# HGRN2 scores as sixteen 32x32 diagonal chunks, and values multiplied chunk by chunk

## The chip, the cores and the metric

The kernel runs on one core of one Trainium2 chip. The metric is the device time of one execution in microseconds (us). A core has a matrix engine (TensorE, PE in the profile, with its weight loads as PEld), VectorE (DVE), ScalarE (ACT), GpSimd (POOL) and SyncE (SP), which here issues most DMA transfers. Each engine works through its own list of instructions in order; semaphores tie the lists together. PE reads SBUF and writes PSUM, which has eight banks.

## The reference

The program is a two-layer encoder trunk on 512 tokens of 1024 features. Each layer projects the normalised input, sends the columns through four mixers side by side (Hyena, Mamba2, dilated attention, HGRN2), projects their outputs back and adds them; then comes a mixture of 16 experts. The change touches HGRN2 alone, whose core is a gated linear attention in chunks of 32 tokens, run once forwards and once backwards, with 4 heads of 64:

```
q, k, v, g = rs(q), rs(k), rs(v), rs(g)          # 16 chunks of 32 tokens
gc = jnp.cumsum(g, axis=2)
ref = gc[:, :, H_CHUNK // 2 - 1:H_CHUNK // 2]
scores = jnp.einsum("bclhe,bcshe->bchls", q * jnp.exp(gc - ref), k * jnp.exp(ref - gc))
scores = jnp.where(mask, scores, 0.0)            # mask: lower triangle, 32 x 32
o_intra = jnp.einsum("bchls,bcshp->bclhp", scores, v)
...
o_inter = jnp.einsum("bclhe,bchep->bclhp", q * jnp.exp(gc), prev)
return (o_intra + o_inter).reshape(b, L, h, pd)
```

Scores join only tokens of one chunk; what comes from earlier chunks comes through the state `prev`. The two directions are added, normalised and gated.

## The kernel before

The 512 tokens stand in four blocks of 128 (b = 0 to 3), each with four chunks of 32 (cc = 0 to 3). The 256 HGRN2 features stand in two halves i of 128 partitions, each with two heads h of 64. The function `hgrn` goes over i. For a half it first prepares the decayed q and k of both directions e (`hgrn_decay`: tiles gqk, and gqi for the part that meets the state), turns k (line 1133), makes the chunk states (1141) and scans them over the chunks on VectorE (1151, 1153) into gR.

Then, for each head h, it makes the scores of each direction: four matmuls of 128x128, one for a block, into one PSUM bank (line 1162, tile gsc). Only the four 32x32 squares on the diagonal of each 128x128 result are wanted. GpSimd clears a page (1164, tile gP), VectorE copies the wanted entries into it under the mask `hmask` (1165), and adds the pages of the two directions (1168). For each block, one matmul with 128 rows multiplies the page with the values of the block (1171), which opens the sum in the output bank go, and for each of its chunks one or two matmuls add the state's part (1178): these have 64 rows (the head's features) and 32 columns (the chunk's tokens), so that the four chunks of a block use four separate column strips of PE's array. The first chunk has no state before it and the last none behind it.

All matmuls here are fp32. In the trace each leaves two records of a weight load and two of a matmul.

The order of the work: `hgrn` is a generator that yields weights, and `weave` interleaves it with `mamba_proj`, the projection for the next mixer (lines 395 to 397 and 417 to 419, tiles pcm and ptm), 40 against 31. A scheduler turns the program into a list for each engine, so the yields move where projection matmuls stand between those of `hgrn`. There is no other table of orders for this stage. After the mixers of a layer, `pieces` streams the expert weights (tile we, line 1391) on the SP queue into buffers that the mixers gave up.

Of the kernel before, what the change touches and what calls it, by code (L numbers as in the profile page):

```python
# [20 lines left out]
P = 128  # L21
# [17 lines left out]
def shape_constants():  # L39
    f32 = np.float32  # L40
    p = np.arange(P)
    c = np.zeros((P, C_N), f32)
    c[:, C_ID:C_ID + P] = np.eye(P)
    c[:, C_LE:C_LE + P] = p[:, None] <= p[None, :]
    c[:, C_GE:C_GE + P] = p[:, None] >= p[None, :]
    c[:, C_IOTA:C_IOTA + 64] = np.arange(1, 65)
    c[:, C_TOK:C_TOK + 4] = 2 * (P * np.arange(4)[None, :] + p[:, None])
    c[:, C_HALF] = p >= 64
    c[:, C_KEY] = 1.0 / KEY
    c[:, C_KEY + 1] = 1.0  # L50
    c[:, C_SLOT] = p % 64 + 1
    same = (p[:, None] // 32) == (p[None, :] // 32)
    m = np.zeros((P, 2, P), np.int32)
    m[:, 0] = same & (p[:, None] <= p[None, :])
    m[:, 1] = same & (p[:, None] >= p[None, :])

    eo = np.concatenate([np.arange(0, L, 2), np.arange(1, L, 2)])
    f = 2.0 * np.pi * (np.arange(P, dtype=np.float64) + 0.5) / (2 * L)  # L60
    n = np.arange(L).reshape(P, 4).T
    th = n[:, :, None] * f
    dft = np.stack([np.cos(th), np.sin(th)]).astype(f32)
    idft = np.ascontiguousarray(dft.transpose(0, 1, 3, 2))
    tk = [eo[:, None] * f, eo[:, None] * (np.pi / 2 - f)]
    kdft = np.stack([np.concatenate([np.cos(tk[0]), np.cos(tk[1])], axis=1),
                     np.concatenate([np.sin(tk[0]), -np.sin(tk[1])], axis=1)])
    kdft = (kdft * (2.0 / (2 * L))).astype(f32)

    t = np.linspace(0.0, 1.0, L, dtype=f32)[:, None]  # L70
    ang_pos = (f32(2.0 * math.pi) * np.arange(L, dtype=f32) / f32(L)).astype(f32)
    bands = np.linspace(1e-4, 15, 16, dtype=f32)
    ang = (ang_pos[:, None] * bands[None, :]).astype(f32)
    z = np.concatenate([t, np.cos(ang), -np.sin(ang)], axis=-1).astype(f32)
    lo = math.log(1e-2) / 1.5
    hi = math.log(1e-2) / 0.3
    deltas = np.abs(np.linspace(lo, hi, 256, dtype=f32))
    decay = np.exp(-t * deltas[None, :]).astype(f32)[eo]

    d = np.arange(511, -512, -1)  # L80
    n = np.abs(d)
    nf = np.maximum(n, 1).astype(f32)
    large = 8 + (np.log(nf / f32(8)) / f32(math.log(128.0)) * f32(8)).astype(np.int32)
    bucket = (d > 0) * 16 + np.where(n < 8, n, np.minimum(large, 15))
    mult = (n <= 64).astype(int) + ((n <= 256) & (n % 4 == 0)) + (n % 16 == 0)
    oh = np.zeros((33, 1024), f32)
    oh[bucket, np.arange(1023)] = 1.0
    oh[32, :1023] = np.where(mult > 0, np.log(np.maximum(mult, 1)), -1e30)
    return {
        "c_pack": c, "c_hmask": m, "c_dft": dft, "c_idft": idft, "c_kdft": kdft,  # L90
        "c_zT": np.ascontiguousarray(z.T), "c_decay": decay, "c_bucket": oh,
    }
# [18 lines left out]
def encoder(ctx: ExitStack, tc: tile.TileContext, d, out, dbg=None, stages=None, nlayers=NL):  # L111
    nc = tc.nc
    V, A, G, T, SY = nc.vector, nc.scalar, nc.gpsimd, nc.tensor, nc.sync
# [33 lines left out]
    def bank_b(name):  # L147
        return tagged(psb, "b", [512], F32, name)

    def page(shape, name, dt=F32):  # L150
        return tl("G", shape, name, dt)
# [68 lines left out]
    ps = bank_b("nmT")  # L220
# [896 lines left out]
    def hgrn(l, st, cols, lb):  # L1117
        q, f, v, g = st
        ve = hgrn_values(v)
        keep = page([2, L], "keep", BF)  # L1120
        G.memset(keep, 1.0)
        G.memset(keep[:, 0, 0::32], 0.0)
        G.memset(keep[:, 1, 31::32], 0.0)
        yield 2
        po = [bank_b("go") for _ in range(2)]
        pov = [p.rearrange("p (b i c) -> p b i c", b=4, i=2) for p in po]
        for i in range(2):
            qk, qi, bes = yield from hgrn_decay(l, i, q, f, lb, keep)
            R = [tl("B", [64, 16], "gR") for _ in range(2)]
            for e in range(2):  # L1130
                ps = bank_b("gkT")
                for b in range(4):
                    T.transpose(ps[:, b * P:(b + 1) * P], qk[1][:, e, b * P:(b + 1) * P], ident)
                kT = page([4, P], "gkT")
                A.activation(kT, ps.rearrange("p (b c) -> p b c", b=4), AF.Copy)
                pu = [bank_b("gU") for _ in range(2)]
                for b in range(4):
                    for z in range(2):
                        a = slice(64 * z, 64 * z + 64)
                        for h in range(2):  # L1140
                            T.matmul(pu[z][64 * h:64 * h + 64, b * P:(b + 1) * P], kT[a, b, 64 * h:64 * h + 64],
                                     ve[b][a, 2 * i + h], start=True, stop=True)

                U, w = tl("B", [64, 16], "gU"), tl("B", [64, 16], "gw")
                for z in range(2):
                    A.activation(U.rearrange("p n (b z c) -> p z b c n", z=2, c=2)[:, z],
                                 pu[z].rearrange("p (b c n) -> p b c n", b=4, n=64), AF.Copy)
                A.activation(w, bes[e][:, None, :].to_broadcast([P, 64, 16]), AF.Copy)
                u, r, w = (x.rearrange("p n c -> p (n c)") for x in (U, R[e], w))
                if e == 0:  # L1150
                    V.tensor_tensor_scan(r, w, u, 0.0, ALU.mult, ALU.add)
                else:
                    V.tensor_tensor_scan(r[:, ::-1], w[:, ::-1], u[:, ::-1], 0.0, ALU.mult, ALU.add)
                yield 2.5
            for h in range(2):
                s = slice(64 * h, 64 * h + 64)
                Ps = []
                for e in range(2):
                    ps = bank_b("gsc")
                    for b in range(4):  # L1160
                        c = slice(b * P, (b + 1) * P)
                        T.matmul(ps[:, c], qk[1][s, e, c], qk[0][s, e, c], start=True, stop=True)
                    w = page([4, P], "gP")
                    G.memset(w, 0.0)
                    V.copy_predicated(w, hmask[:, e, None, :].to_broadcast([P, 4, P]),
                                      ps.rearrange("p (b c) -> p b c", b=4))
                    Ps.append(w)
                V.tensor_add(Ps[0], Ps[0], Ps[1])
                yield 2
                for b in range(4):  # L1170
                    T.matmul(pov[h][:, b, i], Ps[0][:, b], v[:, b, (2 * i + h) * 64:(2 * i + h + 1) * 64],
                             start=True, stop=False)
                    for cc in range(4):
                        c = 4 * b + cc
                        for e in range(2):
                            p = c - 1 if e == 0 else c + 1
                            if 0 <= p < 16:
                                T.matmul(pov[h][32 * cc:32 * cc + 32, b, i], qi[s, e, 32 * c:32 * c + 32],
                                         R[e][s, :, p], start=False, stop=(e == 1 or c == 15))
                    yield 0.8  # L1180
        gs = tl("B", [4, 256], "ggs")
        silu_inplace(g, gs, gs)
        y = tl("B", [4, 256], "gy")
        ss = small([2, 8], "gss")
        for h in range(2):
            sq = page([8, 64], "gsq")
            A.activation(sq, po[h].rearrange("p (n c) -> p n c", c=64), AF.Square)
            V.reduce_sum(ss[:, h], sq, axis=AX.X)
        r = small([16], "grr")
        rsqrt(r, ss.rearrange("p h n -> p (h n)"), 64, "g")  # L1190
        for h in range(2):
            yv = y.rearrange("p b (i h c) -> p b i h c", i=2, h=2)[:, :, :, h]
            V.tensor_mul(yv, pov[h],
                         r.rearrange("p (h b i) -> p h b i", h=2, b=4)[:, h, :, :, None].to_broadcast([P, 4, 2, 64]))
        V.tensor_mul(y, y, gs)
        mix_tile(3)
        for i in range(2):
            ps = bank_b("gyT")
            for b in range(4):
                T.transpose(ps[:, b * P:(b + 1) * P], y[:, b, i * P:(i + 1) * P], ident)  # L1200
            mix_put(3, i, ps, cols[:, R_HGN:R_HGN + 1])
        yield 4
# [432 lines left out]
```

## Time and profile before

| what | value |
|---|---|
| three timed runs | 1661.7, 1661.99, 1667.71 us (median 1661.99) |
| the profiled execution | 1665.74 us, span 1664.0 us |
| granted PE clock, mean over the span | 0.972 of full |
| PE busy | 1536.9 us (92%), 8899 matmul records |
| VectorE busy | 805.7 us (48%) |
| ScalarE, GpSimd busy | 396.1 us, 214.0 us |
| DMA | 468.55 MB, mean 282 GB/s |

The span runs from the first to the last instruction. Busy time of PE counts its pipelined records, whose ends are modelled, so two records can overlap and a busy PE need not be at its peak. The stages lie twice in the span, once for each layer: norm and HGRN2 projection, HGRN2 with Mamba2's projection, Mamba2 with Hyena's, Hyena with attention's, attention, router, experts. PEclk is the clock that PE was granted: 1.00 stands for 2.4 GHz and 0.50 for 1.2 GHz.

### The profile page before, as it was taken

To read this page: it belongs to the slowest core of one execution; us is meant where nothing else is said; L and a number is where in the kernel's file an instruction comes from. 1 tells how busy PE (TensorE), PEld (TensorE's weight loads), DVE (VectorE), ACT (ScalarE), POOL (GpSimd) and SP (SyncE) were. 2 spreads that over 40 slices of the span, in tenths; PEclk is the share of its full clock that TensorE was granted. 3 is DMA by queue.
4 is the path that set the end of the run, shared out by engine and by line. 5 is a ranking of instruction groups with operands and counts; after the bars stand their busy time and mean duration, and the time that the engine had idled before them with its cause. 6 is when DMAs were issued, how large, how long until landed. Compare 5 with 4: busy or idle time off the path is not lost.

```text
span 1664.0 us, 22783 instructions
## 1 busy us (share of the span) xinstructions
PE 1536.9 (92%) x8899; PEld 879.6 (53%) x8899; DVE 805.7 (48%) x1727; ACT 396.1 (24%) x805; POOL 214.0 (13%) x214
## 2 busy tenths in 40 slices
PE   7989999989999998998889999999899999999985
PEld 6778788763433433332368788787534433332332
DVE  6777777562433342331266767856533433332323
ACT  4344434430001010000152435243200001000012
POOL 3232132000000000000033232300000000000001
PEclk9989999989999999999989889999899999999998
DMA  5411224679999999999912202167799999999995
GB/s 165 129 51 28 75 76 162 237 265 369 421 419 422 420 421 420 420 422 420 385 54 80 74 26 77 55 231 261 256 402 419 420 421 420 421 420 420 420 421 239
DMA packets 153486, 468.55 MB, mean 282 GB/s; under 512 B 20408, under 2 KB 56664, under 8 KB 144418
## 3 DMA queue, kind: packets, MB, share of 16 engines
q1 hardware_dynamic: 144742, 455.10, 69.8%
q0 software_dynamic: 2240, 7.34, 1.1%
q10 hardware_dynamic: 6396, 4.65, 0.8%
q8 instruction: 70, 1.15, 0.3%
q14 instruction: 38, 0.31, 0.0%
HBM read 460.60 MB, written 6.44 MB: 281 GB/s over the span
## 4 chain that ended last, share of the span: by engine, by line
PE 61%; DMA 25%; DVE 6%; ACT 3%; issue 2%; POOL 2%; ACTq 0%; SPq 0%; DVEq 0%; POOLq 0%
DMA we<-in_moe_w_up_dram 10%; PE eg L1399 9%; DMA we<-in_moe_w_down_dram 7%; PE eu L1399 7%; PE ey L1399 7%; DMA we<-in_moe_w_gate_dram 6%; PE pcm L395 3%; PE pcm L396 3%; PE pcm L397 3%; PE ec L1470 3%; PE po L1220 2%; PE po L1221 2%; PE po L1222 2%; PE ptm L418 2%; PE ptm L417 2%
## 5 line engine op out<-in xcount | busy, mean ns | idle before, releaser
L1399 PE MATMUL eu<-we,exT 128*64 128x512 f32 x1024 | 239.4, 599 | 20.3 <-DMA we<-in_moe_w_up_dram 18.4
L1399 PE MATMUL ey<-we,ehT 128*64 128x512 f32 x1024 | 232.9, 598 | 18.8 <-ACT ehT L1435 11.5
L1399 PE MATMUL eg<-we,exT 128*64 128x512 f32 x1024 | 231.2, 597 | 10.6 <-DMA we<-in_moe_w_gate_dram 5.9
L1399 PEld LDWEIGHTS eu<-we,exT 128*64 128x64 f32 x1024 | 67.0, 136 | 187.2 <-issue 87.9
L1301 DVE SCALAR_TENSOR_TENSOR ra<-er,ra,tie 128x512 bf16<-128x512 f32 x128 | 95.9, 749 | 135.4 <-PE er L1309 132.5
L1399 PEld LDWEIGHTS ey<-we,ehT 128*64 128x64 f32 x1024 | 69.0, 136 | 157.9 <-issue 96.3
L1399 PEld LDWEIGHTS eg<-we,exT 128*64 128x64 f32 x1024 | 68.8, 136 | 151.4 <-issue 107.3
L1452 DVE SCALAR_TENSOR_TENSOR eY<-ey,erg,eY 64x512 fp32r<-64x512 f32 x64 | 48.0, 749 | 205.3 <-ACT eY L1451 205.2
L1420 ACT ACTIVATE eh<-eg 128x512 f32<-128x512 f32 x32 | 19.1, 598 | 505.3 <-PE eg L1399 505.3
L397 PE MATMUL pcm<-hT,whl 128*128 128x512 f32 x320 | 128.9, 403 | 3.5 <-DVE whl L381 3.5
L396 PE MATMUL pcm<-hT,whl 128*128 128x512 f32 x320 | 130.3, 407 | 0.0
L395 PE MATMUL pcm<-hT,whl 128*128 128x512 f32 x320 | 130.1, 406 | 0.0
L1471 DVE TENSOR_TENSOR x<-x,ec 128x512 f32<-128x512 f32 x128 | 79.8, 682 | 102.8 <-PE ec L1470 102.8
L1346 POOL DMA_INDIRECT exe<-xd,erow x28 | 27.8, 994 | 783.2 <-DVE erg L1327 526.6
L1451 ACT ACTIVATE eY<-ey,erg 64x512 fp32r<-64x512 f32 x64 | 43.7, 683 | 269.4 <-PE ey L1399 245.0
L1427 DVE TENSOR_TENSOR eh<-eh,eu 128x512 f32<-128x512 f32 x32 | 22.0, 688 | 158.7 <-PE eu L1399 158.7
L417 PE MATMUL ptm<-wtm,hT 128*128 128x256 f32 (+1 forms) x256 | 76.5, 300 | 1.7 <-DVE aqs L924 1.7
L1470 PE MATMUL ec<-eY,eot 128*128 128x512 f32 x256 | 67.3, 405 | 10.2 <-DVE erow L1344 6.4
L418 PE MATMUL ptm<-wtm,hT 128*128 128x256 f32 (+1 forms) x256 | 74.6, 293 | 1.3 <-DVE wtm L381 1.3
L380 POOL TENSOR_SCALAR whl<-wraw 128x1024 fp32r<-128x1024 f32 x40 | 46.7, 1169 | 222.1 <-PE pcm L397 113.8
L419 PE MATMUL ptm<-wtm,hT 128*128 128x256 f32 (+1 forms) x256 | 73.7, 291 | 0.0
L397 PEld LDWEIGHTS pcm<-hT,whl 128*128 128x128 f32 x320 | 62.4, 195 | 18.3 <-DVE whl L381 3.9
(386 smaller groups left out, 2381.4 us busy)
## 6 DMA issues: line engine op xcount, KB each, us to landing
we<-in_moe_w_gate_dram SPq DMA_DIRECT2D x216, 512.0 KB
we<-in_moe_w_up_dram SPq DMA_DIRECT2D x208, 512.0 KB
we<-in_moe_w_down_dram SPq DMA_DIRECT2D x204, 512.0 KB
wraw<-in_w_in_dram SPq DMA_DIRECT2D x27, 1024.0 KB
we<-in_moe_w_down_dram SPq DMA_DIRECT2D x26, 1024.0 KB
we<-in_moe_w_up_dram SPq DMA_DIRECT2D x24, 1024.0 KB
we<-in_moe_w_gate_dram SPq DMA_DIRECT2D x20, 1024.0 KB
wo<-in_w_out_dram SPq DMA_DIRECT2D x8, 1024.0 KB
```

Source lines behind the costliest of these rows:

```text
L380: G.tensor_scalar(dst_hi, raw, 1.0, 0.0, op0=ALU.mult, op1=ALU.add)
L395: T.matmul(ps, w[:, 0, k, :], H[k], start=(k == 0), stop=False)
L396: T.matmul(ps, w[:, 0, k, :], Lo[k], start=False, stop=False)
L397: T.matmul(ps, w[:, 1, k, :], H[k], start=False, stop=(k == 7))
L417: T.matmul(dst, h, w[:, 0, k % 4], start=(k == 0), stop=False)
L418: T.matmul(dst, h, w[:, 1, k % 4], start=False, stop=False)
L419: T.matmul(dst, g, w[:, 0, k % 4], start=False, stop=(k == 7))
L1301: V.scalar_tensor_tensor(g, pr, ra[:, c, e, 0:1], tie[:, 384 - c * P:896 - c * P], op0=ALU.subtract, op1=ALU.is_gt, accum_out=k)
L1399: T.matmul(ps[f][64 * f:64 * f + 64], xT[:, j, h], qs[4 * h + j][:, f * 512:(f + 1) * 512], start=(h == 0 and j == 0), stop=(h == 1 and j ...
L1452: V.scalar_tensor_tensor(lo, src, w[c, 0:1], hi.bitcast(F32), op0=ALU.mult, op1=ALU.subtract)
L1470: T.matmul(ps, ot[:, t * P:(t + 1) * P], Y[i][q][n], start=(q == 0), stop=(q == 1))
L1471: V.tensor_add(xrow(t)[:, c], xrow(t)[:, c], ps)
```

## The change

The scores are computed for the sixteen 32x32 squares alone, for each head and direction: 64 matmuls of 64 rows, 32 columns and 32 moving columns for a half i, in place of 16 matmuls of 128x128. Both heads are done in one go. A head has one bank now, with direction e in columns 128 e to 128 e + 127: chunk cc of block b lies on partitions 32 cc to 32 cc + 31, in columns 32 b to 32 b + 31. So the bank is packed, one page w holds both heads and both directions, there are two masked copies of 256 columns and one addition for a half, and the mask is laid out to match.

The page has no zeros between chunks any more, so the value matmul goes chunk by chunk: 32 rows (the chunk's tokens), 32 columns, 64 moving columns, on the row and column strip cc. Each is followed by the state matmuls of its chunk. The yields change from 2 + 4 x 0.8 for a head to 3 for a half and 4 x 1 for a head.

```diff
@@ -49,10 +49,10 @@
     c[:, C_KEY] = 1.0 / KEY
     c[:, C_KEY + 1] = 1.0
     c[:, C_SLOT] = p % 64 + 1
-    same = (p[:, None] // 32) == (p[None, :] // 32)
-    m = np.zeros((P, 2, P), np.int32)
-    m[:, 0] = same & (p[:, None] <= p[None, :])
-    m[:, 1] = same & (p[:, None] >= p[None, :])
+    m = np.zeros((P, 2, 4, 32), np.int32)
+    m[:, 0] = ((p % 32)[:, None] <= np.arange(32))[:, None]
+    m[:, 1] = ((p % 32)[:, None] >= np.arange(32))[:, None]
+    m = m.reshape(P, 2, P)
@@ -1152,32 +1152,37 @@
                 else:
                     V.tensor_tensor_scan(r[:, ::-1], w[:, ::-1], u[:, ::-1], 0.0, ALU.mult, ALU.add)
                 yield 2.5
+
+            pc = [bank_b("gsc") for _ in range(2)]
+            for e in range(2):
+                for c in range(16):
+                    b, cc = divmod(c, 4)
+                    t = slice(32 * c, 32 * c + 32)
+                    for h in range(2):
+                        s = slice(64 * h, 64 * h + 64)
+                        T.matmul(pc[h][32 * cc:32 * cc + 32, P * e + 32 * b:P * e + 32 * b + 32], qk[1][s, e, t],
+                                 qk[0][s, e, t], start=True, stop=True)
+            w = page([2, 2, P], "gP")
+            G.memset(w, 0.0)
+            for h in range(2):
+                V.copy_predicated(w[:, h], hmask, pc[h][:, :256].rearrange("p (e c) -> p e c", e=2))
+            V.tensor_add(w[:, :, 0], w[:, :, 0], w[:, :, 1])
+            yield 3
             for h in range(2):
                 s = slice(64 * h, 64 * h + 64)
-                Ps = []
-                for e in range(2):
-                    ps = bank_b("gsc")
-                    for b in range(4):
-                        c = slice(b * P, (b + 1) * P)
-                        T.matmul(ps[:, c], qk[1][s, e, c], qk[0][s, e, c], start=True, stop=True)
-                    w = page([4, P], "gP")
-                    G.memset(w, 0.0)
-                    V.copy_predicated(w, hmask[:, e, None, :].to_broadcast([P, 4, P]),
-                                      ps.rearrange("p (b c) -> p b c", b=4))
-                    Ps.append(w)
-                V.tensor_add(Ps[0], Ps[0], Ps[1])
-                yield 2
                 for b in range(4):
-                    T.matmul(pov[h][:, b, i], Ps[0][:, b], v[:, b, (2 * i + h) * 64:(2 * i + h + 1) * 64],
-                             start=True, stop=False)
                     for cc in range(4):
                         c = 4 * b + cc
+                        t = slice(32 * cc, 32 * cc + 32)
+                        o = pov[h][t, b, i]
+                        T.matmul(o, w[t, h, 0, 32 * b:32 * b + 32], v[t, b, (2 * i + h) * 64:(2 * i + h + 1) * 64],
+                                 start=True, stop=False)
                         for e in range(2):
                             p = c - 1 if e == 0 else c + 1
                             if 0 <= p < 16:
-                                T.matmul(pov[h][32 * cc:32 * cc + 32, b, i], qi[s, e, 32 * c:32 * c + 32],
-                                         R[e][s, :, p], start=False, stop=(e == 1 or c == 15))
-                    yield 0.8
+                                T.matmul(o, qi[s, e, 32 * c:32 * c + 32], R[e][s, :, p], start=False,
+                                         stop=(e == 1 or c == 15))
+                    yield 1
         gs = tl("B", [4, 256], "ggs")
         silu_inplace(g, gs, gs)
         y = tl("B", [4, 256], "gy")
```

On PE, at the scores of the first half in the first layer, the list before was as follows (gU the chunk states, gsc_1102 and gsc_1110 the two directions of head 0, pcm the projection):

```order
L1141 MATMUL gU_1079<-gve_895,gkT_1076 64x128 x2
L1162 MATMUL gsc_1102<-gqk_956,gqk_957 128x128 x4
L1162 MATMUL gsc_1110<-gqk_956,gqk_957 128x128 x4
L396 MATMUL pcm_1125<-hT_127,whl_1122 128x512
L397 MATMUL pcm_1125<-hT_123,whl_1122 128x512
```

In the list of the changed kernel the same place begins like this (gsc_1102 is head 0, gsc_1103 head 1):

```order
L1141 MATMUL gU_1079<-gve_895,gkT_1076 64x128 x2
L1163 MATMUL gsc_1102<-gqk_956,gqk_957 32x32
L1163 MATMUL gsc_1103<-gqk_956,gqk_957 32x32
L1163 MATMUL gsc_1102<-gqk_956,gqk_957 32x32
L1163 MATMUL gsc_1103<-gqk_956,gqk_957 32x32
```

The two heads alternate, 64 matmuls in a row, before the projection goes on.

At the first value block, still on PE, before (go_954 is the output bank of head 0, gR_1038 and gR_1039 the states of the two directions, gsc_1195 a score bank of head 1):

```order
L397 MATMUL pcm_1125<-hT_124,whl_1122 128x512
L1171 MATMUL go_954<-gv_260,gP_1107 128x64
L1162 MATMUL gsc_1195<-gqk_956,gqk_957 128x128 x3
L1178 MATMUL go_954<-gR_1039,gqi_958 32x64
L1178 MATMUL go_954<-gR_1038,gqi_958 32x64
L1178 MATMUL go_954<-gR_1039,gqi_958 32x64
L1178 MATMUL go_954<-gR_1038,gqi_958 32x64
L1178 MATMUL go_954<-gR_1039,gqi_958 32x64
L1178 MATMUL go_954<-gR_1038,gqi_958 32x64
L1178 MATMUL go_954<-gR_1039,gqi_958 32x64
L1171 MATMUL go_954<-gv_260,gP_1107 128x64
```

The same block in the changed kernel's list on PE, where L1178 is now the value matmul of a chunk and L1183 the state matmul:

```order
L397 MATMUL pcm_1264<-hT_121,whl_1261 128x512
L1178 MATMUL go_954<-gv_260,gP_1168 32x64
L1183 MATMUL go_954<-gR_1039,gqi_958 32x64
L1178 MATMUL go_954<-gv_260,gP_1168 32x64
L1183 MATMUL go_954<-gR_1038,gqi_958 32x64
L1183 MATMUL go_954<-gR_1039,gqi_958 32x64
L1178 MATMUL go_954<-gv_260,gP_1168 32x64
```

One value matmul stood ahead of the state matmuls of four chunks; now one stands ahead of those of each chunk, and this goes on for the 16 chunks of a head. In the first half of a layer projection matmuls stand between the two heads; in the second half the 16 chunks of head 1 follow those of head 0 directly.

## Rows read from the trace of the kernel before

**Rows 1.** The page: busy time by engine, and the chain that ended last.

```profile
PE 1536.9 (92%) x8899; PEld 879.6 (53%) x8899; DVE 805.7 (48%) x1727; ACT 396.1 (24%) x805; POOL 214.0 (13%) x214
...
PE 61%; DMA 25%; DVE 6%; ACT 3%; issue 2%; POOL 2%; ACTq 0%; SPq 0%; DVEq 0%; POOLq 0%
```

**Rows 2.** Windows by stage: busy us and count by engine, PE clock, DMA, GB/s.

```profile
95.00:198.00 103.00, 94.86 (x814) 77.26 (x813) 81.09 (x143) 42.60 (x72) 26.30 (x28) 0.90 0.17 52
...
912.00:1014.00 102.00, 96.70 (x805) 78.91 (x803) 74.04 (x129) 40.23 (x66) 25.95 (x24) 0.88 0.17 53
...
345.00:835.00 490.00, 453.86 (x2389) 182.98 (x2387) 166.82 (x415) 59.80 (x121) 25.78 (x30) 0.99 0.99 400
1165.00:1664.00 499.00, 449.97 (x2375) 181.78 (x2373) 171.24 (x427) 62.28 (x120) 29.02 (x32) 0.98 0.96 390
```

**Rows 3.** Waits of the SP queue, 198 to 345: total us, times, longest.

```profile
SPq L1391 <- PE alog L967: 16.4, 5, 14.2
```

**Rows 4.** Waits of PE for masked scores, 905 to 1160: total us, times, longest.

```profile
PE go L1171 <- DVE gP L1168: 3.8, 2, 2.7
```

**Rows 5.** Timeline of PE, first layer: start, length, line, rows x columns, count.

```profile
127.84 0.43 PE L1171 MATMUL go<-gv,gP 128*128 128x64 f32 x2
128.20 0.67 PE L1178 MATMUL go<-gR,gqi 64*32 64x64 f32 x16
128.80 0.43 PE L1171 MATMUL go<-gv,gP 128*128 128x64 f32 x2
...
130.11 0.65 PE L1178 MATMUL go<-gR,gqi 64*32 64x64 f32 x14
130.69 0.49 PE L1162 MATMUL gsc<-gqk,gqk 64*128 64x128 f32 x2
```

**Rows 6.** The same, start of a whole value block and what follows it.

```profile
137.62 0.33 PE L1171 MATMUL go<-gv,gP 128*128 128x64 f32 x2
...
141.30 0.39 PE L417 MATMUL ptm<-wtm,hT 128*128 128x264 f32 x1
```

**Rows 7.** The same, a piece of a value block of the second layer at half clock.

```profile
940.77 0.69 PE L1171 MATMUL go<-gv,gP 128*128 128x64 f32 x2
941.39 0.70 PE L1178 MATMUL go<-gR,gqi 64*32 64x64 f32 x16
942.02 0.69 PE L1171 MATMUL go<-gv,gP 128*128 128x64 f32 x2
```

**Rows 8.** The same, two score groups, at full and at half clock.

```profile
154.52 2.05 PE L1162 MATMUL gsc<-gqk,gqk 64*128 64x128 f32 x16
...
163.75 3.78 PE L1162 MATMUL gsc<-gqk,gqk 64*128 64x128 f32 x16
```

**Rows 9.** The same, 128.19 to 128.25 and 128.86 to 128.87: records by themselves.

```profile
128.00 0.28 PE L1171 MATMUL go<-gv,gP 128*128 128x64 f32 x1
128.20 0.33 PE L1178 MATMUL go<-gR,gqi 64*32 64x64 f32 x4
...
128.58 0.28 PE L1178 MATMUL go<-gR,gqi 64*32 64x64 f32 x1
```

**Rows 10.** Windows of PE in a value block: busy, clock, DMA.

```profile
978.00:980.00 2.00, 2.00 (x40) 0.79 0.04 8
980.00:982.00 2.00, 2.00 (x30) 0.50 0.00 0
```

**Rows 11.** Timeline of PE, dense projection work at full and at half clock.

```profile
136.03 0.39 PE L397 MATMUL pcm<-hT,whl 128*128 128x512 f32 x1
...
136.48 0.39 PE L396 MATMUL pcm<-hT,whl 128*128 128x512 f32 x1
...
947.55 0.63 PE L397 MATMUL pcm<-hT,whl 128*128 128x512 f32 x1
...
951.81 0.41 PE L395 MATMUL pcm<-hT,whl 128*128 128x512 f32 x1
```

**Rows 12.** Line 1165 by itself: durations in ns, min/median/max.

```profile
L1165 DVE COPY_PREDICATED gP<-hmask,gsc x16: 718/732/743, 120.0 to 985.3; 128x512 f32<-128x512 uint8 x16
```

## The prediction

> **What bounds the kernel now.** I read the page's totals first: TensorE (PE) is busy for 92% of the span and the chain that ended last is 61% PE and 25% DMA [rows 1]. Two views by stage tell more than those averages. The edited code runs twice, in the stretches 95 to 198 us and 912 to 1014 us, where PE is busy for 94.86 of 103 us and 96.70 of 102 us while the DMA engines are busy for 17% [rows 2]: there PE sets the pace. The expert stages are different: their DMA share is 0.96 to 0.99 [rows 2]. So the second question is whether time gained or lost in the mixer is swallowed later by the weight stream. It isn't: expert loads on the DMA queue wait for PE's attention work, behind the mixer, whose buffers they take over [rows 3], so the stream moves with PE. What the edit does to PE in these two stretches goes to the end one to one, less what PE idles in them. Of idle time that the edit can touch there are only the waits of the value matmuls for the masked scores, 3.8 us in the second layer [rows 4] and almost nothing in the first.
>
> **What PE does there now.** One fp32 matmul leaves two records in the trace. A layer has four value blocks (two halves i, two heads h). In each, four times over, one 128-row value matmul (two records, L1171) is followed by seven or eight 64x32 matmuls of the carried state (14 or 16 records, L1178). At full clock a piece starts every 0.96 us: 0.36 for the value matmul and 0.60 for the 16 records [rows 5]. A block takes 3.68 us, as from 137.62 to 141.30 [rows 6]. At half clock a piece takes 1.25 instead of 0.96 (940.77 to 942.02) [rows 7]. The eight blocks, read the same way (3.70, 3.68, 3.79, 3.67, 4.91, 3.69, 4.31, 3.67), sum to 31.4 us. A score group of one head takes 1.98 us at full clock and 3.71 at half (lengths 2.05 and 3.78 in the rows, less the 0.07 by which a modelled end overlaps the next start) [rows 8]. The eight groups are 3.71, 2.17, 1.98, 3.71, 1.98, 3.72, 1.98 and 3.71, sum 23.0 us.
>
> The row that decides is what happens where PE goes from one tile shape to another. Within a shape, records overlap: four 64x32 records on four column tiles start between 128.20 and 128.25 [rows 9]. At a change they don't: the last value record starts at 128.00 and the first 64x32 record at 128.20; the last 64x32 record starts at 128.58 and the next value record at 128.80 [rows 9]. Each group's modelled end lies 0.07 us behind the start of the next shape, at every such change. The change costs a drain of 0.20 to 0.21 us. It does so too where the two shapes use other rows of the array: at 130.69 the score matmuls of head 1 (upper 64 rows) follow state matmuls of head 0 (lower 64 rows), and their start is again 0.07 before the end of 130.11 + 0.65 [rows 5].
>
> The Trainium skill, "TensorEngine Tiling (Array Packing)", Key Properties, says that changing the tiling mode, not just the tile, drains TensorE, and lists 32-row and 64-row shapes as different modes. By that rule the new value matmuls pay what the rows above show, which is the sum below. The trace agrees for every pair of shapes that it holds; it holds no 32-row tile.
>
> **The change, part by part.**
>
> *Value and state matmuls.* The value matmul of a block of 128 positions becomes four 32x32 ones, each followed at once by the two state matmuls of its chunk. So a block alternates 16 times between 32x32 and 64x32 where it went 4 times between 128x128 and 64x32: about 32 changes of shape for 8. And all matmuls of a chunk go to the same column tile, so there is nothing to overlap between two drains. Price of a chunk at full clock: second value record 0.12 behind the first (a step in one tile: 16 records on four tiles are four in a row each, 0.38 from first start to last, so at most 0.13 a step; the 128-row pair shows 0.16); drain 0.20; three steps between four state records 0.34; drain 0.21. That is 0.87 us. The first and last chunk have one state matmul, 0.23 less each: 16 x 0.87 - 0.46 = 13.5 us a block. At half clock the 64x32 group is 0.03 longer and the 128-row pair 0.26 longer (0.63 and 0.62, [rows 7]); a 32x32 tile should be nearer to the small one, so I add 0.08: 14.7 us. The granted clock already fell from full to 0.50 in the course of one value block, 0.79 at 978 to 980 and 0.50 after [rows 10], and stretches four times as long will see it fall more often. I take 14.3, in all 8 x 14.3 - 31.4 = **+83 us**. Bounds: steps of 0.10 and drains of 0.20 at full clock, 12.5 a block, +69; half clock throughout with the whole 0.26, 18 a block, +113.
>
> *Scores.* For each half, 64 matmuls of 32 columns (128 records) on eight 64x32 tiles replace 16 of 128 columns. All have one shape and the heads write two banks, so no drain stands between them. Bounds for a record: 0.013 us (four starts within 0.05, [rows 9]) and 0.037 (16 records in 0.60, four tiles, [rows 5]), so 1.7 to 4.8 us a half. The shape of [rows 5] is the same and has half as many tiles in flight: I take 0.025, 3.2 us, four times 12.8 instead of 23.0: **-10 us** (-16 to -4).
>
> *Clock after the blocks.* When PE comes back to dense work at half clock it needs some matmuls until the clock rises: from 947.55 to 951.81 ten projection matmuls took 4.26 us; at full clock they start 0.225 apart (136.03 to 136.48 for two), so 2.0 us were lost [rows 11]. Before, that follows three times (also behind 163.75 and 981.45, where fewer matmuls are left), about 4.7 us in all. Now each of six stretches of value blocks (three a layer) should end at half clock: 12 us, **+7** (0 to +10).
>
> *VectorE and GpSimd.* 16 masked copies of 0.73 us [rows 12] become 8 of half the columns, 8 additions as long become 4 of half the columns, 12 of 16 memsets go. By columns that is 17 us of VectorE work down to some 4.5, but it lies beside PE. What reaches the end is the value matmuls' wait, those 3.8 us. The first value matmul now waits for both heads' masks and not for one; behind it on PE stand projection matmuls, and before it as many as cover that (14 of them in the first layer). With PE later, ScalarE and VectorE run ahead. **-3** (-8 to +4).
>
> Sum: 83 - 10 + 7 - 3 = +77. The profiled execution took 1665.74 us for a span of 1664.0; with +77 it would be 1743. The three timed runs have their median at 1661.99, 4 us below it, so I put the changed kernel at **1739 us**.
>
> **Rivals.**
>
> *No drain between 32-row and 64-row tiles* (the other side). Within one shape four column tiles work at once [rows 9]; no row shows a 32-row tile, and such a one may run beside a 64-row one as these do. Then the four chunks of a block of positions run on four column tiles at once, six records in a row each: 6 x 0.114 = 0.68 instead of 0.96, 2.7 a block, 8 x 2.7 - 31.4 = -10. With -10 for the scores and -1 of waits: 1641, and up to 1650 where the waits stay. The Trainium skill, "TensorE: Matmul & The Clock Gate", Part 3, has 16 such small tiles packed into one array run up to 10.6 times as fast; it does not speak of two shapes in turn, and no run here shows it. Against the rival: the 130.69 row [rows 5], a drain across disjoint rows. Change is even where a chunk costs (31.4 + 10) / 128 = 0.32 us. 6%.
>
> *Drain only where the rows overlap.* In half of the chunks the 32 value rows lie outside the head's 64 rows. If those ran on without a drain, at about 0.3 each, a block would take 8 x 0.87 + 8 x 0.3 = 9.4: 8 x 9.4 - 31.4 = +44, less 10, plus 5: 1701. The same row of [rows 5] speaks against it. 7%.
>
> *Dearer than the rows show*: a 32x32 tile that drains like the 128-row pair at half clock (0.35), scores at the slow pace, and the clock down for the whole stage: +113 - 4 + 10 + 4 = +123, 1785. 8%.
>
> *The change doesn't reach PE as written*, say scores or values reordered into groups of one shape. The built order shows the alternation row by row, so under 1%.
>
> **How the numbers follow.** Forecast 78%: 1715 to 1775 by itself. From its low bounds, +69 - 16 + 0 - 8 = +45, and the overlap rival at 1701, to the dear end at 1785, the range is 1698 to 1785 and leaves out the no-drain case and some tails. A difference under 0.5% (8 us) can't be told from none here. Faster by more than that: 0.06, from the first rival. Within: 0.02, where a chunk costs near 0.32. Slower: 0.92.
>
> **What would show it.** In the profile after: value blocks of 13 to 15 us with PE starts 0.2 us apart at every change of shape and four records 0.1 apart between them; granted clock at 0.5 in and behind them; score groups of 128 records in 2 to 5 us; both mixer stretches some 35 to 45 us longer, and the expert stages as long as before. I am wrong if a 32x32 record starts while a 64x32 one is still open, which makes a block shorter than 4 us, or if the expert stage comes out shorter by what the mixer lost.

## The result, and the profile after

The changed kernel takes 1729.24 us (median of 4 runs, 1724.79 to 1731.66) against 1662.1 before: 1.0381 times as long, 95% interval 1.0359 to 1.0404. The forecast was 1739, in a range of 1698 to 1785. The profiled execution is the fastest of the four, 1724.79 us, so spans differ by 59.0 us (1723.0 against 1664.0) where the medians differ by 67.

The page of the changed kernel gives busy time by engine and the chain that ended last; it answers to [rows 1]:

```profile
PE 1595.7 (93%) x9475; PEld 910.1 (53%) x9475; DVE 788.9 (46%) x1715; ACT 394.6 (23%) x805; POOL 211.0 (12%) x202
...
PE 62%; DMA 24%; DVE 6%; ACT 3%; issue 2%; POOL 1%; ACTq 0%; SPq 0%; DVEq 0%; POOLq 0%
```

PE gained 58.8 us of busy time and the span gained 59.0. VectorE lost 17 us of work, of which nothing shows in the span. The added time is all in the mixer stretches of the two layers. The expert stage of the first layer, from its first gate matmul to the first matmul of the next layer's filter, stands in these windows (before, then after; columns as in [rows 2]):

```profile
373.40:831.50 458.10, 427.19 (x2229) 164.76 (x2229) 144.57 (x340) 44.86 (x73) 23.71 (x28) 1.00 1.02 412
```

```profile
407.90:864.40 456.50, 425.38 (x2229) 165.53 (x2229) 144.57 (x340) 44.83 (x73) 23.69 (x28) 1.00 1.02 412
```

It begins 34.5 us later and is 1.6 us shorter; the weight stream kept its 412 GB/s. In the second layer the same stage begins 60.6 us later and is again 1.6 us shorter. The stream absorbed no delay: it moved with PE, as [rows 3] had it.

This is the timeline of PE in the first value block after, at full clock (start, length, line, rows x columns, count), which answers to [rows 5]:

```profile
124.53 0.29 PE L1178 MATMUL go<-gv,gP 32*32 32x64 f32 x2
...
125.29 0.29 PE L1178 MATMUL go<-gv,gP 32*32 32x64 f32 x2
125.51 0.60 PE L1183 MATMUL go<-gR,gqi 64*32 64x64 f32 x4
126.05 0.29 PE L1178 MATMUL go<-gv,gP 32*32 32x64 f32 x2
126.27 0.60 PE L1183 MATMUL go<-gR,gqi 64*32 64x64 f32 x4
126.80 0.41 PE L1178 MATMUL go<-gv,gP 32*32 32x64 f32 x2
127.15 0.63 PE L1183 MATMUL go<-gR,gqi 64*32 64x64 f32 x4
127.71 0.41 PE L1178 MATMUL go<-gv,gP 32*32 32x64 f32 x2
```

Every group's modelled end lies 0.06 to 0.07 us behind the start of the next group (125.29 + 0.29 against 125.51, 125.51 + 0.60 against 126.05): no record of one shape starts beside records of the other, as at the changes of shape in [rows 5]. A chunk takes 0.76 us. From 126.80 on a chunk takes 0.91; the granted clock falls there. The next windows of PE (busy, clock, DMA) show it in the first block and in the 27 us of the two heads of the second half:

```profile
125.00:128.00 3.00, 3.00 (x24) 0.78 0.03 5
128.00:137.20 9.20, 9.20 (x63) 0.50 0.36 114
182.00:206.00 24.00, 24.00 (x156) 0.50 0.14 44
```

The score matmuls of the first half, both heads, and what follows them, answering to [rows 8]:

```profile
115.64 1.55 PE L1163 MATMUL gsc<-gqk,gqk 64*32 64x32 f32 x128
117.12 0.79 PE L396 MATMUL pcm<-hT,whl 128*128 128x512 f32 x1
```

The windows of the four score groups (length, then busy time, clock and DMA as above) show that this one ran at half clock and the other three at full clock:

```profile
115.64:117.12 1.48, 1.48 (x133) 0.50 0.05 11
172.08:173.98 1.90, 1.45 (x130) 1.00 0.00 0
962.84:965.75 2.91, 1.39 (x132) 1.00 0.02 6
1018.95:1020.89 1.94, 1.44 (x129) 1.00 0.05 8
```

At half clock the 128 records took 1.48 us, 0.012 apart, where two groups of 16 took 7.42. At full clock PE idled inside the groups, for 0.45, 1.52 and 0.50 us; without that the records are 0.011 apart, where two groups of 16 took 3.96.

### The profile page after: what moved, and what is told of

The parts are those of the page before. It is cut to its first block, busy times and chain, and to the rows that moved or that the text cites. A ratio compares the mean times of both kernels' runs of the same rounds, so it can differ in the third digit from the quotient of the medians.

```text
span 1723.0 us, 23894 instructions
## 1 busy us (share of the span) xinstructions
PE 1595.7 (93%) x9475; PEld 910.1 (53%) x9475; DVE 788.9 (46%) x1715; ACT 394.6 (23%) x805; POOL 211.0 (12%) x202
## 4 chain that ended last, share of the span: by engine, by line
PE 62%; DMA 24%; DVE 6%; ACT 3%; issue 2%; POOL 1%; ACTq 0%; SPq 0%; DVEq 0%; POOLq 0%
DMA we<-in_moe_w_up_dram 10%; PE eg L1404 9%; PE eu L1404 7%; DMA we<-in_moe_w_down_dram 7%; PE ey L1404 7%; DMA we<-in_moe_w_gate_dram 6%; PE go L1183 4%; PE pcm L395 3%; PE pcm L397 3%; PE pcm L396 3%; PE go L1178 2%; PE ec L1475 2%; PE po L1225 2%; PE po L1226 2%; PE po L1227 2%
## 5 line engine op out<-in xcount | busy, mean ns | idle before, releaser
L1404 PE MATMUL eu<-we,exT 128*64 128x512 f32 x1024 | 237.0, 598 | 19.9 <-DMA we<-in_moe_w_up_dram 17.8
L1404 PE MATMUL ey<-we,ehT 128*64 128x512 f32 x1024 | 232.7, 598 | 18.8 <-ACT ehT L1440 11.7
L417 PE MATMUL ptm<-wtm,hT 128*128 128x256 f32 (+1 forms) x256 | 77.6, 305 | 1.7 <-DVE aqs L924 1.7
L418 PE MATMUL ptm<-wtm,hT 128*128 128x256 f32 (+1 forms) x256 | 76.0, 298 | 1.5 <-DVE wtm L381 1.5
L1183 PE MATMUL go<-gR,gqi 64*32 64x64 f32 x480 | 76.6, 294 | 0.0
L419 PE MATMUL ptm<-wtm,hT 128*128 128x256 f32 (+1 forms) x256 | 75.3, 297 | 0.0
```

Source lines behind the costliest of these rows:

```text
L417: T.matmul(dst, h, w[:, 0, k % 4], start=(k == 0), stop=False)
L418: T.matmul(dst, h, w[:, 1, k % 4], start=False, stop=False)
L419: T.matmul(dst, g, w[:, 0, k % 4], start=False, stop=(k == 7))
L1183: T.matmul(o, qi[s, e, 32 * c:32 * c + 32], R[e][s, :, p], start=False, stop=(e == 1 or c == 15))
L1404: T.matmul(ps[f][64 * f:64 * f + 64], xT[:, j, h], qs[4 * h + j][:, f * 512:(f + 1) * 512], start=(h == 0 and j == 0), stop=(h == 1 and j ...
```

## The experiments

Two theories were put against each other. **A**: the price is paid at each change between the 32-row and the 64-row shape, and is a drain of PE, which lets the open matmuls of one shape all but end before the next shape starts. **B**: it lies in the matmuls themselves, in 32-row tiles or in the chain of a chunk's matmuls on one column strip, whatever shape stands beside them.

**Values of a block first (e1_block).** The same instructions; only their order differs.

```
-                    for cc in range(4):
-                        T.matmul(o, w[t, h, 0, ...], v[t, b, ...])      # value of one chunk
-                        ... its state matmuls
+                    for cc in range(4):
+                        T.matmul(pov[h][t, b, i], w[t, h, 0, ...], v[t, b, ...])
+                    for cc in range(4):
+                        ... the state matmuls of chunk cc
```

> The changed kernel, with the four value matmuls of a block of 128 tokens issued together and the state matmuls of its four chunks behind them: the same instructions, but 8 changes of shape in a value block of a head instead of 32. Theory A (a drain of about 0.22 us at every change between 32-row and 64-row shapes is the cost): a value block takes about 4 us instead of 13.5, so some 1729 - 8 x 9.5 = 1653 us, 1640 to 1660. Theory B (32-row matmuls are dear in themselves, or the chunk's chain on one column strip is what takes the time, whatever the shape): the 32-row matmuls still cost what they did, a block stays above 8 us and the kernel above 1690 us.

Measured: 1639.49 us, 0.9872 of before (0.9840 to 0.9904), half a microsecond below the range given. The value blocks sum to 27.3 us instead of 108.2. The timeline of PE in a block:

```profile
125.38 0.31 PE L1176 MATMUL go<-gv,gP 32*32 32x64 f32 x8
125.62 0.65 PE L1184 MATMUL go<-gR,gqi 64*32 64x64 f32 x16
126.20 0.31 PE L1176 MATMUL go<-gv,gP 32*32 32x64 f32 x8
126.44 0.66 PE L1184 MATMUL go<-gR,gqi 64*32 64x64 f32 x16
```

One round of values and states takes 0.82 us and carries four chunks; in the changed kernel it took 0.76 and carried one. 32-row tiles are not dear in themselves. The first form of B falls.

**One shape, order unchanged (e2_one_shape).**

```
-T.matmul(o, w[t, h, 0, 32 * b:32 * b + 32], v[t, b, ...], start=True, stop=False)
+T.matmul(o, w[s, h, 0, 32 * b:32 * b + 32], v[s, b, ...], start=True, stop=False)
```

> The changed kernel with the order of every instruction kept, but each chunk's value matmul reads the head's 64 rows of the page and of the values in place of the chunk's 32 rows, so that value and state matmuls have one shape, 64x32. It thereby adds products of other tokens to the output; only its time is of use. Theory A (drains at the change of shape): no drain is left, chunks run on four column strips at once, a value block falls from 13.5 to 2.5 to 4 us, the kernel to 1635 to 1655 us. Theory B (chain of a chunk on one column strip): order and strips are as before, so a value block stays at 10 us or more and the kernel above 1700 us.

Measured: 1638.5 us, 0.9866 of before (0.9833 to 0.9899), and 91 us below the changed kernel with every matmul in its old place. The timeline of PE at the start of the first block:

```profile
123.99 0.31 PE L1178 MATMUL go<-gv,gP 64*32 64x64 f32 x4 [2.15 <-DVE gP L1169]
124.10 0.31 PE L1183 MATMUL go<-gR,gqi 64*32 64x64 f32 x2
124.14 0.24 PE L1178 MATMUL go<-gv,gP 64*32 64x64 f32 x1
124.19 0.29 PE L1183 MATMUL go<-gR,gqi 64*32 64x64 f32 x1
```

In these lines value and state records start 0.04 to 0.11 us apart, while earlier ones are open. A block takes 2.6 us and all eight 21.7. The chain of a chunk on one strip is as it was, so the second form of B falls too. The edit also moves the value matmul to other rows of the array. A change of rows within one shape does not cost it: the score matmuls of the two heads use rows 0 to 63 and 64 to 127 in turn, and their records are 0.011 us apart.

**Values only (e3_values_only).** The kernel before, with its 128x128 scores and pages; the value matmul takes the 32x32 squares out of the page.

```
-T.matmul(pov[h][:, b, i], Ps[0][:, b], v[:, b, ...], start=True, stop=False)
 for cc in range(4):
+    T.matmul(pov[h][t, b, i], Ps[0][t, b, 32 * cc:32 * cc + 32], v[t, b, ...], start=True, stop=False)
     ... state matmuls of chunk cc
```

> The kernel before, with only the second half of the change: its 128x128 scores, masks and pages stay, and the values are multiplied chunk by chunk, each chunk's value matmul ahead of its state matmuls. Theory A: value blocks as in the changed kernel, 108 us in all against 31.4, scores 23 us as before, so 1662 + 77 = 1739 us, 1730 to 1748. If instead the packed scores had cost time and the values little, it would come out below 1700 us.

Measured: 1742.81 us, 1.0480 of before (1.0444 to 1.0516). Value blocks 106.8 us, scores 24.0. The two are 76 us longer than before, of the 83 between the medians; the rest is open. So the loss comes with the values and does not need the packed scores. The median lies 13.6 us above that of the changed kernel, and the score groups differ by 24.0 - 8.2 = 15.8.

**Both heads together (e4_heads).** For a block of 128 tokens the values of both heads, then the states of both.

```
 for b in range(4):
+    for h in range(2):
+        for cc in range(4): T.matmul(pov[h][t, b, i], w[t, h, 0, ...], v[t, b, ...])
+    for cc in range(4):
+        for e in range(2):
+            for h in range(2): ... state matmul of chunk cc, direction e, head h
```

> The changed kernel with, for each block of 128 tokens, the value matmuls of both heads issued together and then the state matmuls of both heads: 8 changes of shape for both heads of a half instead of 64, and eight tiles at work in the state part. Theory A: about 4 x 1.25 = 5 us for both heads of a half, four times that is 20 us instead of 108, so 1729 - 88 = 1641 us, 1628 to 1650, and faster than the kernel before. Theory B: above 1680 us.

Measured: 1633.29 us, 0.9833 of before (0.9801 to 0.9865): the fastest of the study. The value blocks sum to 17.8 us. A round in its timeline:

```profile
124.18 0.43 PE L1175 MATMUL go<-gv,gP 32*32 32x64 f32 x16 [2.23 <-DVE gP L1169]
124.53 0.70 PE L1185 MATMUL go<-gR,gqi 64*32 64x64 f32 x28
125.16 0.43 PE L1175 MATMUL go<-gv,gP 32*32 32x64 f32 x16
125.52 0.70 PE L1185 MATMUL go<-gR,gqi 64*32 64x64 f32 x32
```

A round takes 0.98 us and carries eight chunks.

**Two chunks at a time (e6_pairs).** As e1_block, with two chunks to a round.

```
 for b in range(4):
+    for c2 in range(2):
+        for cc in (2 * c2, 2 * c2 + 1): ... value matmul
+        for cc in (2 * c2, 2 * c2 + 1): ... state matmuls
```

> The changed kernel with two chunks at a time: their two value matmuls, then their state matmuls, so 16 changes of shape in a value block of a head, between the 32 of the changed kernel (108 us of value blocks) and the 8 of the kernel that goes block by block (27 us, 1639.5 us). Theory A (a price for each change of shape): the value blocks take the linear place between them, 27 + 81 / 3 = 54 us, and the kernel 1660 to 1673 us. If instead only a chunk standing alone is dear (two strips at work already hide it), it comes out within 5 us of 1640.

Measured: 1675.45 us, 1.0088 of before (1.0069 to 1.0108), 2.5 us above the range given; the value blocks sum to 55.7 us, near the 54 expected. The rounds start 0.78 apart:

```profile
123.49 0.30 PE L1177 MATMUL go<-gv,gP 32*32 32x64 f32 x4 [2.46 <-DVE gP L1169]
123.72 0.61 PE L1185 MATMUL go<-gR,gqi 64*32 64x64 f32 x6
124.27 0.30 PE L1177 MATMUL go<-gv,gP 32*32 32x64 f32 x4
```

Set side by side, with rounds counted over both layers:

| kernel | rounds | chunks in one | value blocks, us | a round at full clock, us | median, us |
|---|---|---|---|---|---|
| changed | 128 | 1 | 108.2 | 0.76 | 1729.24 |
| e6_pairs | 64 | 2 | 55.7 | 0.78 | 1675.45 |
| e1_block | 32 | 4 | 27.3 | 0.82 | 1639.49 |
| e4_heads | 16 | 8 | 17.8 | 0.98 | 1633.29 |

From 128 rounds to 64 a round is worth (108.2 - 55.7) / 64 = 0.82 us, from 64 to 32 it is (55.7 - 27.3) / 32 = 0.89. A round costs about the same with one, two or four strips at work, so the number of rounds sets the time. (The medians were not all taken at one time; those of the kernel before, taken with them, lie between 1659.6 and 1662.1 us.)

**Scores only (e7_scores_only).** The packed scores, with the 128-row value matmul of before. The packed page has to be spread for it.

```
+wz = page([4, P], "gP")
+G.memset(wz, 0.0)
+for cc in range(4):
+    V.tensor_copy(wz[t, :, 32 * cc:32 * cc + 32], w[t, h, 0].rearrange("p (b c) -> p b c", b=4))
 for b in range(4):
+    T.matmul(pov[h][:, b, i], wz[:, b], v[:, b, ...], start=True, stop=False)
```

> The changed kernel's packed scores and masks, but the values multiplied as before, one 128-row matmul for a block; for that the packed page is spread to a cleared 128x128 page by four small VectorE copies a head. From the traces: score matmuls 8 us instead of 23, value blocks 31 as before, some 3 us added for the copies on the way to the value matmuls: 1662 - 15 + 3 = 1650 us, 1642 to 1656. If the saving on the scores were hidden behind other work, it would come out at 1660 or above.

Measured: 1659.1 us, 0.9991 of before (0.9970 to 1.0011): no difference, 9 us above the 1650 expected and 3 above the range. The waits of PE show where the 16 us saved on the scores (7.1 against 23.0) went; first layer, then second, answering to [rows 4]:

```profile
PE go L1179 <- DVE gP L1177: 7.6, 2, 5.2
...
PE go L1179 <- DVE gP L1177: 6.6, 2, 3.7
```

Waiting for the spread pages takes 14.2 us where waiting for the masked scores took 4.1. And the value blocks sum to 37.8 us instead of 31.4, since five of its six stretches now run at half clock; the first of them, in its timeline, has the 0.62 for a value pair of [rows 7]:

```profile
128.71 0.69 PE L1179 MATMUL go<-gv,gP 128*128 128x64 f32 x2
129.33 0.69 PE L1186 MATMUL go<-gR,gqi 64*32 64x64 f32 x16
```

16 saved, 10 and 6 given back.

## Why the prediction was right, step by step

**PE sets the pace in these stretches, and the stream moves along.** Right; the expert windows above show it.

**Drain at every change of shape.** Right, and shown from both sides: without changes of shape and with every instruction in place the cost is gone (e2_one_shape), and it follows the number of rounds (table). The rule of the Trainium skill, "TensorEngine Tiling (Array Packing)", Key Properties, that a change of the tiling mode drains TensorE, holds here for the pair of 32-row and 64-row shapes too. The rows give more than the rule. Of a chunk's 0.76 us the two gaps at the changes make up 0.35: 0.14 from the last value record to the first state record (0.22 between the groups less a step of 0.08 in the pair) and 0.21 back. The other 0.41 is the work of the chunk itself, which the drains keep from overlapping with its neighbours'.

**Value blocks, forecast +83.** Measured 108.2 - 31.4 = +76.8 in the profiled executions. The step of the sum that was mis-sized is the first half of a chunk: a value pair with its drain takes 0.22 at full clock where 0.12 + 0.20 was put, since a 32x32 tile's step (0.08) is shorter than the 64x32 step that it was taken from, and its drain (0.14) shorter than that of the 128-row pair. The state half takes 0.54 (forecast 0.34 + 0.21). At half clock a chunk takes 0.91 (forecast 0.95). Some of the +76.8 is not drain but clock: with every chunk at 0.76 a block would take 16 x 0.76 - 0.46 = 11.7 us and all eight 94 instead of 108 (an estimate; the 0.46 is the prediction's, for the chunks with one state matmul).

**Scores, forecast -10.** Measured 8.2 - 23.0 = -14.7. PE idles in three groups for 2.5 us of the 8.2 (twice for ScalarE's gU, line 1146; for the 1.52 the profile shows no releaser), and the records take 5.8: 0.011 us each, under the lower bound of 0.013. To go by the pace of the four tiles of [rows 5] was too careful, for two reasons. Twice as many tiles are in flight: in e4_heads, with 64 moving columns as in [rows 5], 32 records on eight tiles take 0.63 us (125.52 to 126.15), 0.020 each instead of 0.037. And the score matmuls have 32 moving columns and not 64, on as many tiles of the same shape; the step from 0.020 to 0.011 goes with that, and no run takes it apart further.

**Clock, forecast +7.** The clock fell in every stretch of value blocks, as said. Of the projection matmuls between HGRN2's first transposes and those of its output, 75 started at a granted 0.50 after the change and lost 12.8 us by it, against the 12 forecast (a step to the next start, less 0.23 us for lines 395 to 397 and 0.12 for 417 to 419). What the term had wrong is what it set against this: it counted three such places before, 4.7 us, and there was a fourth, behind the first score group:

```profile
117.80 3.78 PE L1162 MATMUL gsc<-gqk,gqk 64*128 64x128 f32 x16
121.51 0.79 PE L396 MATMUL pcm<-hT,whl 128*128 128x512 f32 x1
122.10 0.63 PE L397 MATMUL pcm<-hT,whl 128*128 128x512 f32 x1
```

With it, 37 matmuls lost 7.8 us before: +5.0. How long the half clock lasts differs from place to place. Behind the first block of the first layer the projection matmuls start 0.43 apart from 138.06 to 140.19, five steps; behind the first of the second layer from 985.39 to 990.08, eleven:

```profile
139.77 0.63 PE L397 MATMUL pcm<-hT,whl 128*128 128x512 f32 x1
140.19 0.47 PE L395 MATMUL pcm<-hT,whl 128*128 128x512 f32 x1
140.51 0.39 PE L396 MATMUL pcm<-hT,whl 128*128 128x512 f32 x1
...
989.65 0.63 PE L397 MATMUL pcm<-hT,whl 128*128 128x512 f32 x1
990.08 0.49 PE L395 MATMUL pcm<-hT,whl 128*128 128x512 f32 x1
990.41 0.40 PE L396 MATMUL pcm<-hT,whl 128*128 128x512 f32 x1
```

**Waits, forecast -3.** Wrong in sign, by little. VectorE's part is shorter, two copies of 0.43 and an addition of 0.43 for a half. But one wait now stands for both heads, and 3.1 and 2.9 us are waited where it was 0.3 and 3.8 ([rows 4] has the second):

```profile
PE go L1178 <- DVE gP L1169: 3.1, 2, 2.1
...
PE go L1178 <- DVE gP L1169: 2.9, 2, 2.0
```

Together 76.8 - 14.7 + 5.0 + 1.9 = 69.0, near the 67 between the medians and 10 above the 59.0 between the spans. From HGRN2's first transposes to the end of attention the two layers are 37.1 and 30.6 us longer, 67.7 together. The other stretches, where nothing was changed, are 8.7 us shorter: PE reached the first transposes 2.1 us earlier, each expert stage is 1.6 shorter, and the rest lies in the router and norm stages. Why they are shorter is open.

The mechanism was right. That the size came out within 10 us is in part luck: three terms came out lower than forecast, by 6, 5 and 2 us, and the waits higher by 5. Of the signs named, the value blocks took 12.9 to 13.8 us where 13 to 15 was named, the score groups were as short as 1.5 us where 2 to 5 was named, and the second layer's 30.6 us lies below the 35 to 45.

**The rivals.** No drain between the shapes: refuted by blocks of 13.5 us on average, with each shape's first start only 0.06 to 0.07 us ahead of the other's modelled end; its price of 2.7 us a block is what e2_one_shape takes (2.6), where there is no change of shape. Drain only where rows overlap: refuted by equal periods. In head 0 the state matmuls use rows 0 to 63; chunk 1 (124.53) lies in those rows and chunks 2 and 3 (125.29, 126.05) outside them, and they take 0.76, 0.76 and 0.75 us. The dear case did not come, as a 32x32 tile drains faster than the 128-row pair and not like it. The order was not regrouped.

## What to carry to other kernels

When small fp32 matmuls of two tile shapes take turns, count the turns, not the matmuls: here a round of 32x32 and 64x32 cost 0.76 us with one chunk in it and 0.98 with eight. Group matmuls of one shape and spread them over all column strips and both row halves before changing; that alone turned a loss of 3.8% into a gain of 1.7%. And look at what new copies stand ahead of the engine that sets the pace: with the scores packed but the values as before, PE's saving of 16 us came to nothing.

## What the runs showed that was not expected

A 32x32 tile's drain at full clock (0.14 us) is shorter than that of 64x32 (0.21) or of 128x128 with the same 64 columns (0.20). Eight 64x32 tiles in one shape took a record of an fp32 matmul with 32 moving columns every 0.011 us at full clock and every 0.012 at half clock. The half clock makes the chunk only 1.2 times as long (0.91 against 0.76) where it makes dense projection work 1.9 times as long (0.43 against 0.23). Opening one sum for all four blocks of a bank, so that a half needs a single round, was not tried.
